# Two encoder layers on one core: attention scores laid in couples of neighbouring PSUM banks, with one maximum and one exponential over 1024 keys

## The chip, the cores and the metric

The kernel runs on one core of a Trainium2 chip. Five engines of that core work from queues of their own: TensorE (PE, with its weight loads shown as PEld) multiplies matrices and writes the results to PSUM; VectorE (DVE) and ScalarE (ACT) work by element and can read PSUM; GpSimd (POOL) works by element on SBUF alone; SyncE (SP) issues the DMAs. PSUM has eight banks here, and the kernel gives each a name and a task. The metric is the device time of one execution in microseconds, the median over several runs. The profile is one further execution, and its own time is its span, from the first instruction to the last.

## The reference

Two sequences, a prompt of 2048 tokens and a sample of 512, go through two layers with the same weights. Half of a layer's width is a pooling mixer, the other half differential attention with four heads of two softmax maps each. The change touches the attention:

```python
def block(qblk):
    s = jnp.einsum('bqhcd,bkhcd->bhcqk', qblk, k, preferred_element_type=jnp.float32) * scale
    p = jax.nn.softmax(s, axis=-1)
    a = p[:, :, 0] - lam * p[:, :, 1]
    return jnp.einsum('bhqk,bkhe->bqhe', a.astype(v.dtype), v)
```

So for each head, each query and each of the maps c = 0 and 1 there is a row of scores over all keys, its maximum, the exponentials, and their sum. The two maps are combined into one before they are multiplied with the values.

## The kernel before

**Stages of a layer.** First come the projections of most tokens (`project`, L238, matmuls at L277 and L249), then attention (`attention`, L393) with the remaining projections and the pooled half of the outputs as filling work, then the outputs (`phase3`, L736). Both layers run so. All engines except SP follow the order in which the program text issues their instructions; a wait inside a queue holds everything behind it.

**Banks.** `bank(tag)` (L71) hands out PSUM tiles in turn: four banks "sc", two "tr", one "ot", one "mm". "sc" serves the projections, the attention's scores and the output products. A bank is taken again when every reader of its last contents is done.

**An attention step** (the loop at L591 to L663) handles four jobs. A job is 128 queries against 512 keys of one map: two matmuls (`score`, L439 and L440) into a bank. A prompt row of 2048 keys is thus four jobs, one whole step; a sample row of 512 keys is one job, and a step has four of them (two query tiles with two maps). While a step writes its scores, the four banks of the step before are exponentiated:

```python
for j in range(4):
    if j < len(jobs): score(*jobs[j])
    if j < len(pend): expo(*pend[j])
    if j < len(jobs): peak(*jobs[j])
    if j == 0: early = turn()
late = turn()
```

`score(j)` of this step takes the bank that `expo(j)` of the step before reads, so PE waits at L439 until ACT is done with it. `peak` (L450) takes the maximum of a bank on DVE into a column of `mx`, and after the fourth L453 makes the negated maximum `nm` of the row, which each exponential (L466) needs as its bias. The exponential also sums its elements; an accumulator read behind it stores the sum in `zc`.

**What else a step does.** `turn` (L596) flips two key tiles of an earlier, combined block with four transposes into a "tr" bank (`flip`, L491); it is called after the first score and after the fourth. `flip_split` splits what was flipped into a high part on ACT (L109, `ath`) and a low part on DVE (L114, `atl`), which frees the bank. `values` (L508) multiplies them with the values into the bank "ot"; those flipped late in the step before come before the filling products, those flipped early after them. `fill` (L1024) issues six products of the filling work. A query block (256 queries of a head) takes four steps, or one for the sample. When its last product is done, `finish` copies the bank "ot" on ACT (L516, `oc`), ahead of the late split; DVE multiplies it with the gate (L519, `mt`); in the next step its square is split (L524, L525 on ACT, L526 on DVE, `shl`), and two matmuls with ones (L533) sum the squares at the end of that step. `combine` (L468) runs on POOL once both maps of a query tile are exponentiated: adds over `zc` (L475), the factor, then a multiplication (L481) and an addition (L482) for each 1024 keys. In the last head the prompt's blocks alternate with the sample's (`blocks`, L566).

Of the kernel before, what the change touches and what calls it, by code (L numbers as in the profile page):

```python
# [20 lines left out]
P = 128  # L21
# [9 lines left out]
TB = 512  # L31
# [24 lines left out]
def trunk_kernel(ctx: ExitStack, tc: tile.TileContext, a, outs):  # L56
# [12 lines left out]
    taken = dict.fromkeys(BANKS, 0)  # L69

    def bank(tag):  # L71
        """the banks of a tag in turn"""
        taken[tag] += 1
        return psum.tile([P, TB], F32, name=f"{tag}{taken[tag] % BANKS[tag]}")
# [31 lines left out]
    def split(hi, lo, src, hi_eng, lo_eng):  # L106
        """hi = src rounded to float32r, lo = src - hi (exact)."""
        if hi_eng is nc.scalar:
            nc.scalar.activation(hi, src, AF.Copy)  # L109
        elif hi_eng is nc.gpsimd:  # L110
            nc.gpsimd.tensor_scalar(hi, src, 1.0, 0.0, op0=ALU.mult, op1=ALU.add)
        else:
            nc.vector.tensor_copy(hi, src)
        lo_eng.tensor_tensor(lo, src, f32(hi), op=ALU.subtract)  # L114
# [32 lines left out]
    def norm_block(l, c, st, tb, ht, xp, hts, early, free=lambda: True, more=None, slow=0):  # L147
        """h of 512 tokens, transposed and split, and their rotary tables; yields between
        small steps"""
# [78 lines left out]
    def load_w(raw, p, hi_eng, lo_eng, later=None):  # L228
        """half the rows of the weights of 256 projection columns, split"""
# [8 lines left out]
    def project(st, tb, kind, pair, w, ht, p, tag, halfway):  # L238
        """a pair of projection chunks for a block of tokens; yields between small steps"""
# [44 lines left out]
    def evacuate(st, sl, kind, pair, sub, ps, cs, raws, p):  # L284
        """what follows on a projection chunk, a small step at a time"""
# [36 lines left out]
    def stream(l, jobs, nxt, hts, p, hook, later):  # L322
        """the projections of a layer: each job is a pair of chunks for some blocks; a
        block yields None between small steps and a chunk's tail; True ends a job"""
# [21 lines left out]
    def pool_block(c, st, tb, u_p, t_p, tag):  # L346
        """the pooled channels of 512 tokens; yields between small steps"""
# [45 lines left out]
    def attention(c, p, po, fill):  # L393
        """software-pipelined: a step fills four banks with scores while the four of the
        step before are exponentiated and finished blocks are multiplied with the values"""
# [38 lines left out]
        def score(s, ch):  # L434
            ps = bank("sc")
            q, m = s["b"]["q"], s["m"]
            ts = slice(s["qt"] * P, (s["qt"] + 1) * P)
            kk = s["b"]["ks"][m][ch // 2][:, ch % 2 * TB : (ch % 2 + 1) * TB]
            nc.tensor.matmul(ps, lhsT=q[:, m, 0, ts], rhs=kk, start=True, stop=False)  # L439
            nc.tensor.matmul(ps, lhsT=q[:, m, 1, ts], rhs=kk, start=False, stop=True)  # L440
            s["ps"].append(ps)

        def peak(s, ch):
            if s["nch"] == 1:
                s["nm"] = small.tile([P, 1], F32, name="nm")
                nc.vector.tensor_reduce(s["nm"], s["ps"][ch], axis=AX.X, op=ALU.max, negate=True)
                return
            if ch == 0:
                s["mx"] = small.tile([P, 4], F32, name="mx")
            nc.vector.reduce_max(s["mx"][:, ch : ch + 1], s["ps"][ch], axis=AX.X)  # L450
            if ch == s["nch"] - 1:
                s["nm"] = small.tile([P, 1], F32, name="nm")
                nc.vector.tensor_reduce(s["nm"], s["mx"][:, : s["nch"]], axis=AX.X, op=ALU.max, negate=True)  # L453

        def expo(s, ch):
            m = s["m"]
            if ch == 0 and m == 0:
                s["b"]["z"][s["qt"]] = small.tile([P, 2, 4], F32, name="zc", bufs=16)
            if s["nch"] == 1:
                if s["qt"] == 0:  # L460
                    s["b"][f"e{m}"] = p[f"e{m}"].tile([P, EH], F32, name=f"e{m}")
                s["e"].append(s["b"][f"e{m}"][:, s["qt"] * TB : (s["qt"] + 1) * TB])
            elif ch % 2 == 0:
                s["e"].append(p[f"e{m}"].tile([P, EH], F32, name=f"e{m}"))
            dst = s["e"][ch // 2][:, ch % 2 * TB : (ch % 2 + 1) * TB]
            nc.scalar.activation(dst, s["ps"][ch], AF.Exp, bias=s["nm"], accum_out=s["b"]["z"][s["qt"]][:, m, ch : ch + 1])  # L466

        def combine(b, qt):  # L468
            s0, s1 = b["sets"][2 * qt], b["sets"][2 * qt + 1]
            nch = s0["nch"]  # L470
            z, w = b["z"][qt], nch // 2
# [12 lines left out]
        def flip(b, unit):  # L484
            """two key tiles of a query block, keys onto the partitions"""
# [43 lines left out]
        def squares(b, sq, shl):  # L529
            """the sums of the squares, on all partitions"""  # L530
# [5 lines left out]
        def scales(b, sq, ps):  # L536
            """per query and head, the factor of its normalisation"""
# [28 lines left out]
        def blocks():  # L566
            """the last prompt head in turn with the sample's heads"""
# [23 lines left out]
        while True:  # L591
# [21 lines left out]
            for j in range(4):  # L613
                if j < len(jobs):
                    score(*jobs[j])
                if j < len(pend):
                    expo(*pend[j])
                if j < len(jobs):
                    peak(*jobs[j])
# [53 lines left out]
    def load_wout(l, p, wo, ks, raws, pools):  # L673
        """output weights, split"""
# [30 lines left out]
    def pooled_outputs(wo, p):  # L705
        """the pooled channels' share of the outputs, a token tile after the other"""
# [20 lines left out]
    def drop(q):  # L727
        """a step of the first of a queue of generators"""
# [3 lines left out]
    def each(q):  # L732
        """a step of all of them"""
        q[:] = [g for g in q if next(g, q) is not q]

    def phase3(l, wo, scaling, pairs, kept, es, nxt):  # L736
        """the outputs; what is left of them is returned for the next layer's begin"""
# [9 lines left out]
        def load(st, t):  # L747
            """what a token tile needs, and its scales on the diagonals of matrices"""
# [419 lines left out]
```

## Time and profile before

| | |
|---|---|
| median of three runs | 3195.07 us (3192.13 to 3199.23) |
| the profiled execution, its span | 3198.0 us |
| mean granted TensorE clock | 0.990 |
| first layer: projections, attention | to about 630 us, to about 1440 us |
| second layer: attention | about 2220 to 3025 us |

The page sums busy times over the whole span, so its shares mix stages with different limits. Of an engine's group of instructions it gives the sum, the mean of one, and the idle time in front of them with what ended it. The timeline gives start and length of single instructions, and in brackets the idle time of their engine before them. A matmul's length is modelled to the end of its way through the array, so neighbours overlap: the spacing of their starts is the time that one really takes of the engine.

### The profile page before, as it was taken

Reading aid. Unit: us, or ns where it says so; the run is one execution under the profiler, and the core shown is the slowest. Engines: PE = TensorE matmul, PEld = TensorE weight load, DVE = VectorE, ACT = ScalarE, POOL = GpSimd, SP = SyncE. Lnnn points to the kernel's source line nnn. Section 1 sums busy time; section 2 is a strip of 40 time slices with the busy share of each in tenths; the row PEclk is TensorE's granted clock in tenths of the full one; section 3 lists DMA queues with packets and bytes.
Section 4 is the critical chain, followed back from the end, with each engine's and each line's share of the span. In section 5 each row is a group of like instructions: output and inputs, shape, how many; then the busy total and the mean of one; then the engine's idle time right before and its main releaser. Section 6 shows DMA issues by size and latency. Waiting matters only on the chain. (4 is left out here: it accounts for less than half of the span.)

```text
span 3198.0 us, 48570 instructions
## 1 busy us (share of the span) xinstructions
PE 3088.4 (97%) x16936; PEld 2601.0 (81%) x16936; DVE 2174.8 (68%) x3289; ACT 1751.7 (55%) x3995; POOL 1856.8 (58%) x2058
## 2 busy tenths in 40 slices
PE   8999999999999999998899999999999999999998
PEld 6898888778887888887688888887788878888876
DVE  3354255588888887877834543555888988877767
ACT  3244233377777777773333442333777777777722
POOL 1000122288998888888820001222989888888888
PEclk9999999999999999999999999999999999999999
DMA  5354357643424334436754544577434243353367
GB/s 199 116 158 145 129 159 207 193 133 98 124 63 133 111 105 133 126 100 237 265 183 118 158 137 137 165 202 214 117 90 122 64 139 112 93 154 111 103 216 241
DMA packets 298902, 464.55 MB, mean 145 GB/s; under 512 B 26144, under 2 KB 180768, under 8 KB 298656
## 3 DMA queue, kind: packets, MB, share of 16 engines
q1 hardware_dynamic: 298656, 461.44, 48.2%
q8 instruction: 134, 2.20, 0.3%
q14 instruction: 112, 0.92, 0.1%
HBM read 293.57 MB, written 167.77 MB: 144 GB/s over the span
## 5 line engine op out<-in xcount | busy, mean ns | idle before, releaser
L450 DVE TENSOR_REDUCE mx<-sc 128x1 f32<-128x512 f32 x1024 | 650.4, 684 | 189.1 <-PE sc L440 187.1
L466 ACT ACTIVATE e<-sc,nm 128x512 f32<-128x512 f32 x1088 | 733.1, 694 | 44.0 <-DVE nm L453 40.0
L482 POOL TENSOR_TENSOR e<-e,e 128x1024 f32<-128x1024 f32 (+1 forms) x288 | 666.2, 2313 | 24.0
L277 PE MATMUL sc<-hth,wh 128*128 128x512 f32 x1408 | 556.0, 395 | 0.0
L277 PE MATMUL sc<-htl,wh 128*128 128x512 f32 x1408 | 554.6, 394 | 0.0
L277 PE MATMUL sc<-hth,wl 128*128 128x512 f32 x1408 | 552.8, 393 | 0.0
L109 ACT ACTIVATE ath<-tr 128x512 fp32r<-128x512 f32 x544 | 327.9, 605 | 236.8 <-PE ot L508 193.5
L439 PE MATMUL sc<-ks,q 128*128 128x512 f32 x1024 | 432.9, 423 | 10.4 <-DMA ks<-ks_p 5.3
L440 PE MATMUL sc<-ks,q 128*128 128x512 f32 x1024 | 406.5, 397 | 0.0
L114 DVE TENSOR_TENSOR atl<-tr,ath 128x512 fp32r<-128x512 f32 x544 | 363.6, 682 | 46.5 <-ACT ath L109 46.3
L508 PE MATMUL ot<-ath,v 128*128 128x256 f32 x2176 | 370.1, 292 | 1.9 <-ACT oc L516 1.9
L491 PE MATMUL tr<-ident,e 128*128 128x128 f32 x2176 | 328.3, 275 | 21.7 <-DVE atl L114 21.3
L491 PEld LDWEIGHTS tr<-ident,e 128*128 128x128 f32 x2176 | 268.5, 141 | 97.9 <-DVE atl L114 34.1
L167 POOL TENSOR_TENSOR rs<-ss,mhalf 128x1 f32<-128x1 f32 x40 | 27.0, 676 | 551.9 <-DVE ss L165 551.8
L481 POOL TENSOR_SCALAR e<-e,nco 128x1024 f32<-128x1024 f32 (+1 forms) x288 | 328.0, 1139 | 15.0
L508 PEld LDWEIGHTS ot<-ath,v 128*128 128x128 f32 x2176 | 312.6, 190 | 22.4 <-ACT oc L516 2.7
L277 PEld LDWEIGHTS sc<-hth,wl 128*128 128x128 f32 x1408 | 264.7, 188 | 59.1
L277 PEld LDWEIGHTS sc<-hth,wh 128*128 128x128 f32 x1408 | 264.8, 188 | 58.5 <-POOL wl L114 0.3
L277 PEld LDWEIGHTS sc<-htl,wh 128*128 128x128 f32 x1408 | 264.9, 188 | 57.6 <-DVE htl L114 0.4
L439 PEld LDWEIGHTS sc<-ks,q 128*128 128x128 f32 x1024 | 194.4, 190 | 64.6 <-ACT e L466 30.8
L114 DVE TENSOR_TENSOR wl<-wr,wh 128x1024 fp32r<-128x1024 f32 x94 | 120.8, 1287 | 182.2 <-ACT wh L109 182.1
L466 ACT ACTIVATION_READ_ACCUMULATOR e<-sc,nm 128x1 f32 x1088 | 231.1, 212 | 0.0
(149 smaller groups left out, 5987.6 us busy)
## 6 DMA issues: line engine op xcount, KB each, us to landing
wr<-in_w_in SPq DMA_DIRECT2D x128, 512.0 KB, 4.2
q<-qs_p SPq DMA_DIRECT2D x128, 256.0 KB, 4.2
ks_p<-hl SPq DMA_DIRECT2D x64, 256.0 KB, 3.5
vs_p<-hl SPq DMA_DIRECT2D x128, 128.0 KB, 2.7
qs_p<-hl SPq DMA_DIRECT2D x64, 256.0 KB, 3.5
mp_p<-hl SPq DMA_DIRECT2D x32, 512.0 KB, 3.8
ks<-ks_p SPq DMA_DIRECT2D x64, 256.0 KB, 5.4
v<-vs_p SPq DMA_DIRECT2D x32, 512.0 KB, 5.5
```

Source lines behind the costliest of these rows:

```text
L109: nc.scalar.activation(hi, src, AF.Copy)
L114: lo_eng.tensor_tensor(lo, src, f32(hi), op=ALU.subtract)
L167: nc.gpsimd.tensor_tensor(rs, ss, mhalf[:, :1], op=ALU.pow)
L277: nc.tensor.matmul(ps, lhsT=w[k // 4][m][:, k % 4, ns], rhs=h[:, k, :], start=k + i == 0, stop=k == KT - 1 and i == 2)
L439: nc.tensor.matmul(ps, lhsT=q[:, m, 0, ts], rhs=kk, start=True, stop=False)
L440: nc.tensor.matmul(ps, lhsT=q[:, m, 1, ts], rhs=kk, start=False, stop=True)
L450: nc.vector.reduce_max(s["mx"][:, ch : ch + 1], s["ps"][ch], axis=AX.X)
L466: nc.scalar.activation(dst, s["ps"][ch], AF.Exp, bias=s["nm"], accum_out=s["b"]["z"][s["qt"]][:, m, ch : ch + 1])
L481: nc.gpsimd.tensor_scalar(x1[:, :n], x1[:, :n], nco, 0.0, op0=ALU.mult, op1=ALU.add)
L482: nc.gpsimd.tensor_tensor(x0[:, :n], x0[:, :n], x1[:, :n], op=ALU.add)
L491: nc.tensor.transpose(ps[:, j, qt * P : (qt + 1) * P], e[kt // 8][:, kt % 8 * P : (kt % 8 + 1) * P], ident)
L508: nc.tensor.matmul(b["ot"][:, :QB], lhsT=b["vs"][v][kt // 8][:, kt % 8, :], rhs=at[:, j, :], start=unit + i == 0, stop=kt == nkt - 1 and i ...
```

## The change

The four "sc" banks become two tiles of two neighbouring banks, `sc0` and `sc1`. `bank("sc")` returns a half of such a couple; a new couple is taken at every second call, and is free only when all readers of both old halves are done. The projections and the output products use the halves as they used banks.

In a step the jobs are handled by twos. Two scores are written, then the couple of the step before is exponentiated, then the maximum of the new couple is taken. For the prompt, maximum and exponential each read 1024 keys of both banks in one instruction; `mx` and `zc` have two columns instead of four, and `combine` adds once instead of twice. For the sample one maximum instruction gives the two maxima of a couple, and the exponentials stay at 512 keys each. The early flip now comes after the second score. The rest of the diff takes comment strings out.

```diff
+    couples = []
     def bank(tag):
-        taken[tag] += 1
-        return psum.tile([P, TB], F32, name=f"{tag}{taken[tag] % BANKS[tag]}")
+        n, taken[tag] = taken[tag], taken[tag] + 1
+        if tag != "sc":
+            return psum.tile([P, TB], F32, name=f"{tag}{n % BANKS[tag]}")
+        if n % 2 == 0:
+            couples[:] = [psum.tile([P, 2, TB], F32, name=f"sc{n // 2 % 2}")]
+        return couples[0][:, n % 2]
...
+        def peak(jobs):
+            s, ch = jobs[0]
+            both = s["ps"][ch]
             if s["nch"] == 1:
+                nm = small.tile([P, 2], F32, name="nm")
+                nc.vector.tensor_reduce(nm, both, axis=AX.X, op=ALU.max, negate=True)
+                for i, (s, _) in enumerate(jobs):
+                    s["nm"] = nm[:, i : i + 1]
                 return
...
-            nc.vector.reduce_max(s["mx"][:, ch : ch + 1], s["ps"][ch], axis=AX.X)
-            if ch == s["nch"] - 1:
+            nc.vector.reduce_max(s["mx"][:, ch // 2 : ch // 2 + 1], both.rearrange("p i n -> p (i n)"), axis=AX.X)
+            if ch == s["nch"] - 2:
...
+        def expo(jobs):
+            for s, ch in jobs:
...
+                    nc.scalar.activation(s["e"][0], s["ps"][0][:, m], AF.Exp, bias=s["nm"], accum_out=z)
+                elif ch % 2 == 0:
+                    s["e"].append(p[f"e{m}"].tile([P, EH], F32, name=f"e{m}"))
+                    src = s["ps"][ch].rearrange("p i n -> p (i n)")
+                    nc.scalar.activation(s["e"][-1], src, AF.Exp, bias=s["nm"], accum_out=z)
...
-            z, w = b["z"][qt], nch // 2
+            z, w = b["z"][qt], nch // 4
...
-            for j in range(4):
-                if j < len(jobs):
-                    score(*jobs[j])
-                if j < len(pend):
-                    expo(*pend[j])
-                if j < len(jobs):
-                    peak(*jobs[j])
+            for j in (0, 2):
+                if jobs:
+                    score(jobs[j : j + 2])
+                if pend:
+                    expo(pend[j : j + 2])
+                if jobs:
+                    peak(jobs[j : j + 2])
                 if j == 0:
                     early = turn()
```

More of the change, by code (lines that the diff above doesn't have):

```diff
@@ L432, in load_q, with score @@
             return q
[L434 to L443, printed above, removed]
+        def score(jobs):
+            for s, ch in jobs:
+                ps = bank("sc")
+                q, m = s["b"]["q"], s["m"]
+                ts = slice(s["qt"] * P, (s["qt"] + 1) * P)
+                kk = s["b"]["ks"][m][ch // 2][:, ch % 2 * TB : (ch % 2 + 1) * TB]
+                nc.tensor.matmul(ps, lhsT=q[:, m, 0, ts], rhs=kk, start=True, stop=False)
+                nc.tensor.matmul(ps, lhsT=q[:, m, 1, ts], rhs=kk, start=False, stop=True)
+                s["ps"].append(couples[0])
@@ L444, in peak @@
+        def peak(jobs):
+            s, ch = jobs[0]
+            both = s["ps"][ch]
             if s["nch"] == 1:
-                s["nm"] = small.tile([P, 1], F32, name="nm")
-                nc.vector.tensor_reduce(s["nm"], s["ps"][ch], axis=AX.X, op=ALU.max, negate=True)
+                nm = small.tile([P, 2], F32, name="nm")
+                nc.vector.tensor_reduce(nm, both, axis=AX.X, op=ALU.max, negate=True)
+                for i, (s, _) in enumerate(jobs):
+                    s["nm"] = nm[:, i : i + 1]
@@ L447, in peak @@
                 return
             if ch == 0:
-                s["mx"] = small.tile([P, 4], F32, name="mx")
-            nc.vector.reduce_max(s["mx"][:, ch : ch + 1], s["ps"][ch], axis=AX.X)
-            if ch == s["nch"] - 1:
+                s["mx"] = small.tile([P, 2], F32, name="mx")
+            nc.vector.reduce_max(s["mx"][:, ch // 2 : ch // 2 + 1], both.rearrange("p i n -> p (i n)"), axis=AX.X)
+            if ch == s["nch"] - 2:
                 s["nm"] = small.tile([P, 1], F32, name="nm")
-                nc.vector.tensor_reduce(s["nm"], s["mx"][:, : s["nch"]], axis=AX.X, op=ALU.max, negate=True)
@@ L455, in expo @@
[L455 to L466, printed above, removed]
+                nc.vector.tensor_reduce(s["nm"], s["mx"], axis=AX.X, op=ALU.max, negate=True)
@@ new lines, in expo @@
+        def expo(jobs):
+            for s, ch in jobs:
+                m = s["m"]
+                if ch == 0 and m == 0:
+                    s["b"]["z"][s["qt"]] = small.tile([P, 2, 2], F32, name="zc", bufs=16)
+                z = s["b"]["z"][s["qt"]][:, m, ch // 2 : ch // 2 + 1]
+                if s["nch"] == 1:
+                    if s["qt"] == 0:
+                        s["b"][f"e{m}"] = p[f"e{m}"].tile([P, EH], F32, name=f"e{m}")
+                    s["e"].append(s["b"][f"e{m}"][:, s["qt"] * TB : (s["qt"] + 1) * TB])
+                    nc.scalar.activation(s["e"][0], s["ps"][0][:, m], AF.Exp, bias=s["nm"], accum_out=z)
[3 more added lines that the diff above has]
+                    nc.scalar.activation(s["e"][-1], src, AF.Exp, bias=s["nm"], accum_out=z)
```

## The prediction

> **What bounds the kernel now.** I read the page first: the span, the busy times, the groups of the two instructions that the change merges.
>
> ```profile
> span 3198.0 us, 48570 instructions
> PE 3088.4 (97%) x16936; PEld 2601.0 (81%) x16936; DVE 2174.8 (68%) x3289; ACT 1751.7 (55%) x3995; POOL 1856.8 (58%) x2058
> ...
> L450 DVE TENSOR_REDUCE mx<-sc 128x1 f32<-128x512 f32 x1024 | 650.4, 684 | 189.1 <-PE sc L440 187.1
> L466 ACT ACTIVATE e<-sc,nm 128x512 f32<-128x512 f32 x1088 | 733.1, 694 | 44.0 <-DVE nm L453 40.0
> ...
> L466 ACT ACTIVATION_READ_ACCUMULATOR e<-sc,nm 128x1 f32 x1088 | 231.1, 212 | 0.0
> ```
>
> TensorE is the bound by its busy share, and the merged instructions lie on VectorE and ScalarE. The next view, busy time by window over two neighbouring attention steps (from one first score load to the next), says what that means here.
>
> ```profile
> 1130.58:1136.13 5.55, 5.55 (x37) 4.84 (x36) 3.93 (x7) 3.85 (x11) 5.38 (x4) 1.00 0.00 0
> 1136.13:1141.67 5.54, 5.54 (x36) 4.83 (x35) 4.21 (x8) 4.53 (x12) 3.30 (x6) 1.00 0.14 50
> ```
>
> The columns are length, then busy PE, weight loads, DVE, ACT, POOL. PE is busy 5.55 of 5.55 us, DVE 3.93, ACT 3.85. Time saved on DVE or ACT is worth nothing in such a step. It counts only where PE waits, so I read the waits of its weight loads next (total us, times, longest).
>
> ```profile
> PEld tr L491 <- DVE atl L114: 34.1, 49, 3.5
> PEld sc L439 <- ACT e L466: 30.8, 78, 1.7
> ...
> PEld tr L533 <- DVE shl L526: 23.6, 34, 2.3
> ```
>
> These 88 us are the waits that the change can touch: 2.8% of the span. It can shorten them, or add to the second.
>
> **The change, part by part.** The prices of a doubled instruction come from the groups that differ in size only.
>
> ```profile
> L109 ACT ACTIVATE woh<-wor 128x512 fp32r<-128x512 f32 x16 | 10.2, 639 | 0.0
> L109 ACT ACTIVATE woh<-wor 128x1024 fp32r<-128x1024 f32 x8 | 8.5, 1068 | 0.0
> L453 DVE TENSOR_REDUCE nm<-mx 128x1 f32<-128x4 f32 x256 | 40.3, 158 | 8.8
> L543 DVE TENSOR_REDUCE v<-sq 128x2 f32<-128x256 f32 x80 | 33.6, 420 | 7.2
> ```
>
> ACT: 512 more elements cost 1068-639 = 0.43 us, so an exponential of 1024 takes about 0.694+0.43 = 1.12. DVE: (684-158)/508 = 1.04 ns an element, so a maximum of 1024 takes 0.684+0.53 = 1.21. Against two of 512 that saves 0.27 and 0.16, and 512 accumulator reads go. No row reads two banks at once. The bounds are therefore no second fixed cost at all (these prices) and nothing saved (1.39 and 1.37). I take the first, whose rows have the same sizes. The change removes no matmul and no DMA. POOL loses one 0.2 us add for each combine.
>
> Now the latency, in the quiet step.
>
> ```profile
> 1132.27 1.89 DVE L450 TENSOR_REDUCE mx<-sc 128x1 f32<-128x512 f32 x3 [0.21 <-PE sc L440]
> ...
> 1132.54 0.39 PE L439 MATMUL sc<-ks,q 128*128 128x512 f32 x1
> ...
> 1132.76 0.40 PE L440 MATMUL sc<-ks,q 128*128 128x512 f32 x1
> ...
> 1134.11 0.60 ACT L109 ACTIVATE ath<-tr 128x512 fp32r<-128x512 f32 x1 [1.70 <-PE ot L508]
> ...
> 1134.19 0.16 DVE L453 TENSOR_REDUCE nm<-mx 128x1 f32<-128x4 f32 x1
> ...
> 1134.60 0.68 ACT L466 ACTIVATE e<-sc,nm 128x512 f32<-128x512 f32 x1
> ...
> 1135.17 0.20 ACT L466 ACTIVATION_READ_ACCUMULATOR e<-sc,nm 128x1 f32 x1
> ...
> 1136.13 0.19 PEld L439 LDWEIGHTS sc<-ks,q 128*128 128x128 f32 x1
> ```
>
> The last score ends at 1133.16. Today the first bank is free when the accumulator read ends, 1135.37, and PE returns at 1136.13: 0.76 us of cover. Afterwards the second maximum starts at 1133.20 and ends at 1134.41, the combined one at about 1134.61, the exponential starts at 1134.65, its accumulator read (0.57+0.43 later) ends at 1135.85. Cover 0.2 to 0.3 us: **no loss, but little left**. Behind the waiting score load stand all of PE's later flips and products, so a wait beyond the cover is lost whole.
>
> In one step of each query block a finished output (L516) comes between, and there the cover is too small.
>
> ```profile
> L516 ACT ACTIVATE oc<-ot 128x256 f32<-128x256 f32 x80 | 30.8, 385 | 110.4 <-PE ot L508 110.4
> ```
> ```profile
> 1139.45 0.40 PE L508 MATMUL ot<-atl,v 128*128 128x256 f32 x2
> ...
> 1139.89 0.39 ACT L516 ACTIVATE oc<-ot 128x256 f32<-128x256 f32 x1 [1.01 <-PE ot L508]
> ...
> 1140.17 0.59 ACT L109 ACTIVATE ath<-tr 128x512 fp32r<-128x512 f32 x1
> ...
> 1140.65 0.69 ACT L466 ACTIVATE e<-sc,nm 128x512 f32<-128x512 f32 x1
> ...
> 1141.22 0.21 ACT L466 ACTIVATION_READ_ACCUMULATOR e<-sc,nm 128x1 f32 x1
> 1141.31 0.70 ACT L466 ACTIVATE e<-sc,nm 128x512 f32<-128x512 f32 x1
> ...
> 1141.67 0.19 PEld L439 LDWEIGHTS sc<-ks,q 128*128 128x128 f32 x1
> ```
>
> PE's product, the copy and the split hold the exponential to 1140.65 whatever the maxima do. Its read ends at 1141.43 now, 1141.86 after; PE asks at 1141.67, and a load follows a release by 0.05 us (1254.39 to 1254.44, below). So PE waits 0.24. Of the 64 prompt blocks the 48 of the first three heads have this step, two of them in a stretch without cover: 46 x 0.24 = **11 us lost** (0 to 23 between the bounds: a read that ends as early as today, and a doubled fixed cost, 0.24+0.26 each).
>
> In the last head the step before is the sample's. It keeps exponentials of 512, and a couple is free only after both.
>
> ```profile
> 1253.77 0.19 PEld L439 LDWEIGHTS sc<-ks,q 128*128 128x128 f32 x1 [0.37 <-ACT e L466]
> ...
> 1254.16 0.23 ACT L466 ACTIVATION_READ_ACCUMULATOR e<-sc,nm 128x1 f32 x1
> ...
> 1254.44 0.19 PEld L439 LDWEIGHTS sc<-ks,q 128*128 128x128 f32 x1 [0.37 <-ACT e L466]
> ```
>
> PE already follows the exponentials here; only the fourth score comes behind the fourth exponential. Afterwards the third does too: two matmuls at the 0.23 us spacing of 1132.54 and 1132.76, 0.46 us, in 14 such steps: **6 us lost**.
>
> Where PE has few filling products the loop through ACT and DVE sets the pace already.
>
> ```profile
> 653.38 0.19 PEld L439 LDWEIGHTS sc<-ks,q 128*128 128x128 f32 x1
> ...
> 657.82 0.19 PEld L439 LDWEIGHTS sc<-ks,q 128*128 128x128 f32 x1 [0.33 <-ACT e L466]
> ```
>
> 4.44 us a step. After: release to third score load 0.05, four matmuls 0.12+3x0.23+0.40, maximum 0.04+1.21, combined one 0.04+0.16, second exponential 0.04+(0.66+0.43) later (0.66 from 1140.65 to 1141.31, the spacing today), its read's end 1.20 after that: 5.0. About ten steps in both layers lie so, each at 0 to 0.6: **5 us lost**. Losses: 22.
>
> Gains. Flips wait for their bank (L491). The first flip moves behind the second score, 2 x 0.23 = 0.46 us later on PE, while the splits that free banks come 0.25 later in quiet steps.
>
> ```profile
> 1102.89 0.35 PEld L491 LDWEIGHTS tr<-ident,e 128*128 128x128 f32 x3 [0.18 <-DVE atl L114]
> ```
>
> Some 17 waits of this size vanish (3 us), and twelve of 0.8 to 3.5 lose 0.2 to 0.5 each: **7 us gained** of 34 (0 to 15). The second gain is at the squares.
>
> ```profile
> L475 POOL TENSOR_TENSOR zc<-zc 128x4 f32<-128x4 f32 x128 | 30.2, 236 | 58.5 <-ACT e L466 58.5
> ```
> ```profile
> 1099.55 2.41 POOL L482 TENSOR_TENSOR e<-e,e 128x1024 f32<-128x1024 f32 x1
> ...
> 1100.17 2.06 DVE L526 TENSOR_TENSOR shl<-sq,shl 128x256 fp32r<-128x256 f32 x1
> ...
> 1102.29 0.19 PEld L533 LDWEIGHTS tr<-shl,ones 128*128 128x128 f32 x1 [0.64 <-DVE shl L526]
> ```
>
> The DVE subtraction of 256 elements takes 2.06 us: it ends 0.27 after POOL's add that began before it. POOL's chain of adds starts at the latest accumulator read (L475 waits for it), in the quiet step at 1134.60+3x0.66+0.77 = 1137.35 now and at 1134.65+1.09+1.20 = 1136.94 after, 0.4 us earlier, and is one add shorter (0.24), 0.6 in all; this subtraction starts about 0.25 later in its step, and the step itself 0.24 later. Most of the collision is then over. Of the 23.6 us some 6 lie after the last scores; of the rest I take three quarters: **13 us gained** (0 to 17, or below: a new collision costs 0.64 a block).
>
> Elsewhere the couples cost nothing: a chunk of the projections waits for the evacuation of the chunk three back, not four, with two chunks of 24 matmuls x 0.23 = 11 us of cover, and L782's products have 12 x 0.23 x 2 = 5.5 us. Without that cover it would be one 0.6 us evacuation a time. At the start of a layer's attention the third score, not the fourth, waits for the last evacuation of the projections: 0.2 us, twice, which is in the rounding.
>
> Sum: 22 lost, 20 gained, **+2 us** on the span of 3198.0, which stands 2.9 above the median of the runs. On the median 3195.1: **3197**.
>
> **The rivals.** *Faster: the relief of the engines arrives in full.* All waits on DVE above, less 9 us after the last scores, are 49; if two thirds go and the losses are half of mine, 11-33 = -22: 3173; with all losses 3184. For it: 68% DVE, backlogged in the steps with long waits. Against it: quiet steps have no DVE wait at all. The Trainium skill ("Advanced Engine Details and Errata", The Read-Write Bubble) advises 512 or 1024 elements and one instruction over several banks; no wider read is in this trace yet.
>
> *Slower: coarser release, and the collision stays.* If the subtraction starts inside POOL's add after the change too, the 13 us don't come: 3197+13 = 3210; if every one of the 46 blocks collides at 0.64, +29 more. It decides as soon as the subtraction starts before POOL's add ends. For it: both starts move by amounts of the same size, and only the difference counts. The Trainium skill ("Perfetto Trace Analysis", Optimizing Scalar/DVE Operations) says that engines that are not full but cause bubbles elsewhere are helped by breaking instructions up; the 0.76 us of cover agree with it, as merging takes 0.5 of them.
>
> *It doesn't do what it says*: a read over two banks pays twice. Then the 11 become 23, and of the quiet steps the two in each of 46 blocks that have no squares behind them lose what their cover of 0.28 lacks against 0.27+0.16: 92 x 0.15 = 14. 3197+26 = 3223. Against it: the accumulator read and the fixed cost are seen once for each instruction here, and 256 to 512 elements already cost by the element on DVE.
>
> **How the numbers follow.** A measurement of this kernel tells 0.2%, 6.4 us, from no change. My forecast, losses and gains that cancel, 3197: 0.41. Coarse release 0.29 and double price 0.05: slower 0.34. Full relief: faster 0.25. Both signs together hold more than the forecast, whose own range is 3189 to 3201. The 80% range reaches from the rival with all losses and a little beyond, 3180, to between the slower ones, 3218.
>
> **What would show it.** Right: 512 exponentials of 128x1024 at about 1.12 us, maxima at 1.21; PE's waits for e at L439 up from 30.8 by some 20 us, in steps with an L516; L533's waits for shl well down; period of the quiet step still 5.55. Wrong: the quiet step grows (cover misjudged); exponentials of 1.39 us; shl waits that grow (the POOL phase); or PE busy falling with no named wait.

## The result, and the profile after

The changed kernel takes 3477.36 us (median of 4 runs, 3470.42 to 3483.95), the kernel before in the same comparison 3195.49 us (4 runs, 3192.13 to 3199.23). The ratio is 1.0883, 95% interval 1.087 to 1.0897: **slower by 8.8%**, far outside the predicted 3180 to 3218. Two of the runs below, the maximum alone and the exponential alone, each had one slow execution among four (11330.82 and 11864.49 us); their ratios leave it out.

The line numbers of the changed kernel are some lines further down. Those used here: the projections' matmuls are L282 (L277 before) and, for the values, L254; the copies that take a projection chunk out of its bank L294, L301, L307 (all `ra`) and L263; the outputs' matmuls L796 (L782) with their evacuation L799; scores L446 and L447, maximum L461, exponential L480 (L476 for the sample), flips L505, copy of a finished output L530, squares L547.

First the head of the page of the changed kernel, with the groups of the two merged instructions.

```profile
span 3468.6 us, 47211 instructions
PE 3159.9 (91%) x16936; PEld 2629.2 (76%) x16936; DVE 2121.9 (61%) x2745; ACT 1663.7 (48%) x2971; POOL 1793.2 (52%) x1930
...
L461 DVE TENSOR_REDUCE mx<-sc 128x1 f32<-128x1024 f32 x512 | 622.0, 1222 | 248.9 <-PE sc L447 219.8
L480 ACT ACTIVATE e<-sc,nm 128x1024 f32<-128x1024 f32 x512 | 566.6, 1114 | 47.4 <-DVE nm L464 45.3
```

The span grew by 270.6 us. (The medians are 281.9 apart: the profiled execution of the changed kernel lies 6.9 us under its median and the span of the kernel before 2.9 over its own, so differences of the two profiles come out some 11 us small.) The merged instructions cost what was expected of them (1.222 and 1.114 us), VectorE, ScalarE and GpSimd all have less to do than before, and TensorE has the same 16936 matmuls. But TensorE stands idle for 3468.6 - 3159.9 = 308.7 us instead of 109.6, and the time in which any of its matmuls runs is 71.5 us longer.

Where is that? Busy time by window, cut at the first and last score of each layer: the columns are the window, its length, then busy time (and instructions) of PE, weight loads, DVE, ACT, POOL, the granted clock, the DMA share and GB/s. The kernel before:

```profile
0.00:633.00 633.00, 617.38 (x3097) 519.20 (x3098) 298.25 (x395) 223.16 (x356) 96.46 (x116) 1.00 0.54 163
633.00:1435.00 802.00, 779.37 (x4708) 665.93 (x4707) 665.64 (x1118) 603.83 (x1548) 687.91 (x765) 0.99 0.40 113
1435.00:2223.00 788.00, 763.42 (x3764) 633.46 (x3763) 422.94 (x524) 272.39 (x451) 238.06 (x261) 0.99 0.58 179
2223.00:3022.00 799.00, 776.20 (x4707) 663.94 (x4706) 662.20 (x1118) 603.31 (x1547) 687.35 (x763) 0.99 0.40 114
3022.00:3198.00 176.00, 151.99 (x668) 118.45 (x666) 125.78 (x135) 49.03 (x96) 146.96 (x156) 0.95 0.67 217
```

The changed kernel:

```profile
0.00:740.00 740.00, 640.60 (x3097) 524.18 (x3098) 294.01 (x395) 224.36 (x356) 93.23 (x116) 0.97 0.46 140
740.00:1550.00 810.00, 781.99 (x4709) 669.32 (x4708) 645.58 (x848) 558.41 (x1036) 673.02 (x703) 1.00 0.40 112
1550.00:2475.00 925.00, 802.53 (x3765) 649.85 (x3764) 412.82 (x523) 273.75 (x450) 223.86 (x259) 0.96 0.50 153
2475.00:3284.00 809.00, 781.41 (x4706) 668.88 (x4706) 646.56 (x848) 558.58 (x1036) 672.61 (x703) 1.00 0.40 112
3284.00:3468.00 184.00, 153.34 (x664) 116.97 (x662) 122.92 (x133) 48.65 (x95) 130.49 (x153) 0.95 0.63 207
```

The windows hold the same matmuls, within a few. Attention (the second and fourth) grew by 8 and 10 us. The first projections grew by 107, the stretch from the first layer's outputs to the second layer's scores by 137, the last outputs by 8. So **some 250 of the 270 us lie where the change merges nothing**; what reached these stages is only the new shape of the tiles that `bank("sc")` hands out.

The waits of the weight loads in the changed kernel (total us, times, longest) name them.

```profile
PEld sc L282 <- ACT ra L307: 83.2, 32, 7.0
PEld sc L282 <- ACT ra L301: 81.9, 36, 8.6
PEld sc L796 <- DVE y L799: 58.4, 39, 4.7
PEld sc L446 <- ACT e L480: 38.9, 89, 2.9
PEld tr L505 <- DVE atl L119: 33.4, 42, 3.1
PEld sc L282 <- ACT ra L294: 26.1, 20, 4.2
PEld sc L254 <- ACT ra L263: 24.8, 16, 3.5
PEld sc L446 <- ACT e L476: 11.8, 24, 0.6
PEld tr L547 <- DVE shl L540: 9.2, 12, 1.7
```

Before the change no projection matmul into an `sc` bank waited for `ra` or for `y`. Now L282 waits 32 + 36 + 20 = 88 times, 191.2 us in all, L254 24.8 us and L796 58.4 us: 274 us, against 24.3 us of another wait (L782 for hl) that these hide now. That difference, 250 us, is about the loss outside attention.

The number 88 says more. L282 has 3 x 1408 = 4224 matmuls into `sc` banks; at 24 a chunk that is 176 chunks, or 88 couples: **one wait for each couple**. In order of issue, 36 of the waits stand at the first matmul of a couple's second half, 24 at its second and 28 at its third; none stands in a first half. L796's 39 waits are all at the first matmul of a second half, out of 40 couples of 12 matmuls a half. One of them in the timeline (start, length, engine, line; in brackets the idle time before, and what ended it):

```profile
253.15 0.39 PE L282 MATMUL sc<-hth,wh 128*128 128x512 f32 x1
...
253.61 0.39 PE L282 MATMUL sc<-hth,wl 128*128 128x512 f32 x1
253.74 0.69 DVE L319 TENSOR_TENSOR t<-t,t 128x512 f32<-128x512 f32 x1
254.47 0.63 ACT L114 ACTIVATE hl<-t 128x512 fp32r<-128x512 f32 x1 [2.14 <-DVE t L319]
255.00 0.58 ACT L307 ACTIVATE ra<-sc 128x512 f32<-128x512 f32 x1
...
255.63 0.19 PEld L282 LDWEIGHTS sc<-hth,wh 128*128 128x128 f32 x1 [2.06 <-ACT ra L307]
```

The first half of a couple is complete at 254.00. Its evacuation `ra` stands in ScalarE's queue behind a split that waits for VectorE, and ends at 255.58. The second half is another bank, which nobody reads; yet TensorE starts on it only at 255.63. The list of the built program shows the same without any time: a matmul in the middle of a second half waits for a semaphore of ScalarE, whose queue has the evacuation of the same tile (number 368) there; the count that it waits for is the one that this evacuation brings. The two matmuls before it are issued ahead of the evacuation and need not wait, which is why the wait stands at the first, second or third matmul of a half.

```
93 L282 MATMUL sc_368<-htl,wh 128x512
94 L282 MATMUL sc_368<-hth,wl 128x512 [waits Activation_49]
...
24 L294 ACTIVATE ra_422<-sc1_368 128x512 [waits DMAHW0_49,PE_49]
```

**Theory.** A couple is one tile, and the program's order between writers and readers is kept by the tile: writing one half waits for the read of the other half, though these are two banks. In the projections and outputs, where the halves are filled one after the other and each is read out alone, every second chunk waits for the evacuation of the chunk just finished. **Rival A**: it is the coarser release that I had named (a couple comes free only when both halves are read). **Rival B**: the merged attention disturbs what comes after.

### The profile page after: what moved, and what is told of

Its sections match the earlier page's. It is cut to its first block, busy times and chain, and to the rows that moved or that the text cites. A ratio compares the mean times of both kernels' runs of the same rounds, so it can differ in the third digit from the quotient of the medians.

```text
span 3468.6 us, 47211 instructions
## 1 busy us (share of the span) xinstructions
PE 3159.9 (91%) x16936; PEld 2629.2 (76%) x16936; DVE 2121.9 (61%) x2745; ACT 1663.7 (48%) x2971; POOL 1793.2 (52%) x1930
## 5 line engine op out<-in xcount | busy, mean ns | idle before, releaser
L461 DVE TENSOR_REDUCE mx<-sc 128x1 f32<-128x1024 f32 x512 | 622.0, 1222 | 248.9 <-PE sc L447 219.8
L282 PE MATMUL sc<-hth,wh 128*128 128x512 f32 x1408 | 569.8, 405 | 67.9 <-ACT ra L307 36.4
L282 PE MATMUL sc<-hth,wl 128*128 128x512 f32 x1408 | 566.9, 403 | 44.6 <-ACT ra L307 25.3
L282 PE MATMUL sc<-htl,wh 128*128 128x512 f32 x1408 | 567.8, 403 | 41.2 <-ACT ra L301 27.4
L480 ACT ACTIVATE e<-sc,nm 128x1024 f32<-128x1024 f32 x512 | 566.6, 1114 | 47.4 <-DVE nm L464 45.3
L446 PE MATMUL sc<-ks,q 128*128 128x512 f32 x1024 | 436.5, 426 | 25.4 <-ACT e L480 16.6
L447 PE MATMUL sc<-ks,q 128*128 128x512 f32 x1024 | 405.2, 396 | 0.0
L282 PEld LDWEIGHTS sc<-hth,wh 128*128 128x128 f32 x1408 | 271.5, 193 | 141.7 <-ACT ra L307 43.2
L282 PEld LDWEIGHTS sc<-hth,wl 128*128 128x128 f32 x1408 | 271.2, 193 | 116.3 <-ACT ra L307 28.7
L282 PEld LDWEIGHTS sc<-htl,wh 128*128 128x128 f32 x1408 | 271.3, 193 | 109.4 <-ACT ra L301 30.9
L505 PE MATMUL tr<-ident,e 128*128 128x128 f32 x2176 | 327.6, 275 | 20.0 <-DVE atl L119 19.5
L505 PEld LDWEIGHTS tr<-ident,e 128*128 128x128 f32 x2176 | 267.9, 141 | 98.3 <-DVE atl L119 33.4
L796 PE MATMUL sc<-woh,hl 128*128 128x512 f32 x640 | 214.1, 416 | 46.1 <-DVE y L799 41.1
L446 PEld LDWEIGHTS sc<-ks,q 128*128 128x128 f32 x1024 | 193.9, 189 | 76.9 <-ACT e L480 38.9
```

Source lines behind the costliest of these rows:

```text
L282: nc.tensor.matmul(ps, lhsT=w[k // 4][m][:, k % 4, ns], rhs=h[:, k, :], start=k + i == 0, stop=k == KT - 1 and i == 2)
L461: nc.vector.reduce_max(s["mx"][:, ch // 2 : ch // 2 + 1], both.rearrange("p i n -> p (i n)"), axis=AX.X)
L480: nc.scalar.activation(s["e"][-1], src, AF.Exp, bias=s["nm"], accum_out=z)
L505: nc.tensor.transpose(ps[:, j, qt * P : (qt + 1) * P], e[kt // 8][:, kt % 8 * P : (kt % 8 + 1) * P], ident)
L796: nc.tensor.matmul(ps, lhsT=lhsT, rhs=w[:, ns], start=i == 0, stop=i == len(todo) - 1)
```

## The experiments

**Where it sits: each part of the change alone.** The first run keeps couples in attention only. The score banks get a pool of their own, opened anew as single banks or as couples at the borders of attention.

```diff
+        if scores["kind"] == "single":
+            return scores["pool"].tile([P, TB], F32, name=f"sb{n % 4}")
         if n % 2 == 0:
-            couples[:] = [psum.tile([P, 2, TB], F32, name=f"sc{n // 2 % 2}")]
+            couples[:] = [scores["pool"].tile([P, 2, TB], F32, name=f"sc{n // 2 % 2}")]
...
+            lay("couple")
             scaling = attention(c, pa, po, fill)
+            lay("single")
```

> Couples in attention only; projections, poolings and outputs write single 512-wide banks again, as before the change. Theory (a couple is one tile, so matmuls into one half wait until the other half has been read out): the waits of L282 on ra (83.2 + 81.9 + 26.1 us after the change) and of L796 on y (58.4 us) go, the two projection stages fall back to some 634 and 613 us, and the time is about 3213 us (3195 + the 17.6 us that attention lost; 3205 to 3220). Rival A (the couples cost outside attention because a chunk must wait for an evacuation three back): the same time, so this run alone does not tell it from the theory. Rival B (the loss comes from attention or from memory laid out otherwise, and the projections only show it): over 3400 us.

Measured: 3223.29 us, ratio 1.0087 (1.0069 to 1.0105), 3 us above the expected range: attention costs more here than the 17.6 us of the one profile that the forecast went by. The opposite run is the kernel before with its old attention and single banks there, and couple tiles, never used as couples, everywhere else.

> The kernel before with its attention as it was (single banks, maxima and exponentials of 512 keys), but with couple tiles, unused as couples, for the projections, the poolings and the outputs. Theory (a write to one half waits for the read of the other half): 3195 + 107 + 118 + 20 + some 12 of the last outputs = about 3450 us (3430 to 3465), with the same waits of L282's twin on ra and of L796's twin on y in second halves. Rival (the loss needs the change in attention too, by the order of work it hands on): near 3195 us.

Measured: 3457.26 us, ratio 1.0813 (1.0798 to 1.0828). The two parts add up to within 7 us: 28 us from attention alone, 260 from the other stages alone, 282 from both. Rival B is out: the old attention with couples elsewhere shows the same waits to within a few per cent (its L293, L318, L312 and L798, L801 are the changed kernel's L282, L307, L301 and L796, L799).

```profile
PEld sc L293 <- ACT ra L318: 83.0, 32, 7.0
PEld sc L293 <- ACT ra L312: 82.3, 36, 9.0
PEld sc L798 <- DVE y L801: 58.1, 39, 4.7
```

**What it is: tile or release.** The next run keeps the couples in every stage. Outside attention only the order differs in which chunks take the four halves: the first halves of both couples, then the second halves.

```diff
+        if where["crossed"]:
+            if n % 4 < 2:
+                crossed[n % 2] = psum.tile([P, 2, TB], F32, name=f"sc{n % 2}")
+            return crossed[n % 2][:, n // 2 % 2]
         if n % 2 == 0:
```

> Couple tiles everywhere, but outside attention neighbouring chunks go crosswise: first halves of both couples, then second halves. Four banks, and a couple is still taken anew only when both of its halves are read. Theory (writes to one half wait for reads of the other): the chunk that follows an evacuation is in the other tile, so what waits is a chunk two later, a whole chunk (24 x 0.23 = 5.5 us) after the evacuation was queued: most of the 216 us of L282's waits go, 3213 to 3260 us. Rival A (coarse release of a couple): the release is coarser than in the changed kernel, the last half of a couple is read out just before it is needed, so the waits stay or grow: 3470 us or more, with the waits at a first half's first matmul.

Measured: 3228.43 us, ratio 1.0097 (1.008 to 1.0114). What is left of the waits of the projections for `ra` (here L286 and L258), from the crossed run:

```profile
PEld sc L286 <- ACT ra L311: 6.5, 4, 2.1
...
PEld sc L286 <- ACT ra L305: 4.6, 2, 2.4
PEld sc L258 <- ACT ra L267: 2.5, 2, 1.3
```

13.6 us instead of 216.0. The release of a couple is as coarse as ever, or coarser, so rival A predicted no less than 3470 and falls. With neighbouring chunks in different tiles the read of one chunk has the whole next chunk (5.5 us) to itself, and that is enough. At the outputs, where a chunk is only 12 products (2.8 us), it is not quite: L800, the outputs' matmuls of the crossed run, still waits 31.1 us, where the changed kernel has 58.4 for y and the kernel before 24.3 for hl; the view names no releaser for these loads, and for 17.5 us of the matmuls behind them it names y.

**Within attention: which half of the merge costs.** Two runs start from the single-outside run and take one merge back: the maximum alone over 1024 keys (exponentials of 512 each), and the exponential alone.

```diff
-                    src = s["ps"][ch].rearrange("p i n -> p (i n)")
-                    nc.scalar.activation(s["e"][-1], src, AF.Exp, bias=s["nm"], accum_out=z)
+                if s["nch"] > 1:
+                    z = s["b"]["z"][s["qt"]][:, m, ch : ch + 1]
+                    dst = s["e"][ch // 2][:, ch % 2 * TB : (ch % 2 + 1) * TB]
+                    nc.scalar.activation(dst, s["ps"][ch][:, ch % 2], AF.Exp, bias=s["nm"], accum_out=z)
```

> As the single-outside run, but in attention only the maximum runs over 1024 keys; the exponentials run over 512 each (four partial sums again). Theory: the 0.24 us of a step with a finished output come from the long exponential, behind which the copy of the output delays the next one, so they go (11 us), the exponentials of 0.69 us come twice 0.69 - 1.11 = 0.27 us per pair dearer on a ScalarE that is half idle, and the loss of the short-fill stretches is halved: 3195 to 3205 us. Rival: the maximum over 1024 alone sets the loss (the exponential must wait for a 1.22 us maximum instead of 0.68): as slow as with both, 3213 us.

```diff
-            nc.vector.reduce_max(s["mx"][:, ch // 2 : ch // 2 + 1], both.rearrange("p i n -> p (i n)"), axis=AX.X)
+            for i in range(2):
+                nc.vector.reduce_max(s["mx"][:, ch + i : ch + i + 1], both[:, i], axis=AX.X)
```

> As the single-outside run, but in attention only the exponential runs over 1024 keys; the maxima run over 512 each. Theory: the steps with a finished output keep their 0.24 us (11 us), the short-fill stretches get part of theirs back, as the last maximum starts after the last score's bank and takes 0.68 us: 3205 to 3213 us. Rival: the maximum is what costs, and this one is back at 3195 us.

Measured: 3257.53 us (1.019, 1.0173 to 1.0207) and 3233.11 us (1.0111, 1.0094 to 1.0128). Both miss: **neither is faster than both merges together** (3223.29), and the maximum alone is clearly slower. For that one, I had forgotten my own theory. As long as two banks are one tile, the first score of a couple waits for the second exponential, and two of 0.691 us end later than one of 1.115. The waits for e say so, and those of the squares for shl grow nearly as much; single-outside first, then maximum only:

```profile
PEld sc L457 <- ACT e L491: 40.0, 93, 2.9
PEld tr L558 <- DVE shl L551: 12.6, 14, 1.7
```
```profile
PEld sc L457 <- ACT e L493: 56.6, 99, 2.5
PEld tr L560 <- DVE shl L553: 26.1, 39, 2.4
```

So with couples in place merging the exponential pays (34 us, 3257.53 against 3223.29). Merging the maximum as well may pay a little (10 us, 3233.11 against 3223.29), but the intervals of these two runs overlap. Neither run says what single banks would do; that is the order-only run below.

**The 0.24 us of a step with a finished output.** Two ways to take the copy `oc` out of the way of the long exponential. First onto VectorE, in the single-outside run and, as a control, in the kernel before:

```diff
-            nc.scalar.activation(oc, ot[:, :QB], AF.Copy)
+            nc.vector.tensor_copy(oc, ot[:, :QB])
```

> As the single-outside run (3223 us), and the copy of a finished output out of its bank (the oc line) runs on VectorE, no longer on ScalarE between two long exponentials. Theory (the 0.24 us of 46 steps with a finished output and part of the 0.49 us of the 14 sample steps come from this copy delaying a long exponential): these steps go back to 5.55 us, 11 to 18 us less than the single-outside run, 3205 to 3212 us. Rival (the second exponential is late because its maximum ends late, whatever stands in ScalarE's queue): the steps keep 5.79 us, and the time stays at 3223 us.

> Control: the kernel before with the same copy on VectorE. Its exponentials of 0.69 us left room for the copy, so theory expects no change, 3190 to 3202 us. If the copy on ScalarE cost the kernel before something too, it would be under 3185 us.

Measured: 3240.9 us (1.0133, 1.0119 to 1.0147) and 3219.56 us (1.0069, 1.0055 to 1.0082). Both miss, and the control says why the pair can't decide: the move by itself costs the kernel before 23 us. In such a step of the run, from the timeline, the exponential is early, at 988.37 in a step that began at 984.30 (4.07 us in, where the single-outside run has 4.53), but the products of the next block wait until the copy, now behind the maxima and a split in VectorE's queue, has left their bank:

```profile
988.37 1.11 ACT L491 ACTIVATE e<-sc,nm 128x1024 f32<-128x1024 f32 x1
988.85 0.41 DVE L541 COPY oc<-ot 128x256 f32<-128x256 f32 x1
...
989.38 0.53 PEld L533 LDWEIGHTS ot<-ath,v 128*128 128x128 f32 x4 [0.39 <-issue]
```

A cleaner way leaves the copy on ScalarE and changes only its place: the split of the second flip, whose data are there earlier, goes ahead of it.

```diff
-            for g in finishing:
-                next(g)
             if late:
                 flip_split(late[2])
                 flipped.append(late)
             for g in finishing:
                 next(g)
+            for g in finishing:
+                next(g)
```

> As the single-outside run (3223 us), with one order changed: the split of the second flip of a step (ath on ScalarE, atl on VectorE) is issued ahead of the copy oc of a finished output, not behind it. In the single-outside run oc waits 1.49 us for its products in front of that ath and the exponential, which starts 4.53 us into such a step although its maximum is there at 4.02. Theory (ScalarE's queue makes the long exponential late in these steps, and its end releases the couple 0.24 us late): the exponential starts some 0.3 to 0.4 us earlier, these 46 steps go back to 5.55 to 5.6 us without burdening VectorE, and the time falls by 8 to 15 us, to 3208 to 3215 us. Rival (something else of these steps, such as the later maximum or the copy's place on whichever engine, costs the 0.24): 3220 us or more.

> Control: the kernel before with the same order of split and copy. Its first bank is free after 0.69 us of exponentials, 5.21 us into a step of 5.55, so theory expects no gain from an earlier exponential: 3190 to 3200 us.

Measured: 3207.33 us (1.0035, 1.0022 to 1.0049), 16 us less than the single-outside run and just past the expected range, and for the control 3197.1 us (1.0007, 0.9998 to 1.0016), the kernel before unchanged. The same step in the timelines, the single-outside run first (its step begins at 977.56):

```profile
981.33 0.39 ACT L541 ACTIVATE oc<-ot 128x256 f32<-128x256 f32 x1 [1.49 <-PE ot L533]
...
981.61 0.59 ACT L125 ACTIVATE ath<-tr 128x512 fp32r<-128x512 f32 x1
982.09 1.12 ACT L491 ACTIVATE e<-sc,nm 128x1024 f32<-128x1024 f32 x1
...
983.35 0.19 PEld L457 LDWEIGHTS sc<-ks,q 128*128 128x128 f32 x1 [0.15 <-ACT e L491]
```

With the split first (its step begins at 972.57):

```profile
976.10 0.60 ACT L125 ACTIVATE ath<-tr 128x512 fp32r<-128x512 f32 x1 [1.25 <-PE ot L533]
...
976.59 0.38 ACT L541 ACTIVATE oc<-ot 128x256 f32<-128x256 f32 x1
976.86 1.12 ACT L491 ACTIVATE e<-sc,nm 128x1024 f32<-128x1024 f32 x1
...
978.13 0.19 PEld L457 LDWEIGHTS sc<-ks,q 128*128 128x128 f32 x1
```

The exponential starts 4.29 us into the step instead of 4.53, and the next score load comes after 5.56 us, without a wait, instead of 5.79. The 0.24 us are ScalarE's order in front of a long exponential, as the prediction said.

In the sample's steps half of the loss stayed (5.80 us from score load to score load; 5.54 before, 6.03 after). One more run gives each of the sample's score sets a maximum of its own:

```diff
-                nm = small.tile([P, 2], F32, name="nm")
-                nc.vector.tensor_reduce(nm, both, axis=AX.X, op=ALU.max, negate=True)
                 for i, (s, _) in enumerate(jobs):
-                    s["nm"] = nm[:, i : i + 1]
+                    s["nm"] = small.tile([P, 1], F32, name=f"nm{i}")
+                    nc.vector.tensor_reduce(s["nm"], both[:, i], axis=AX.X, op=ALU.max, negate=True)
```

> The run with the split first (3207 us, 1024 keys an instruction), with the maxima of the sample's steps taken over 512 keys each, one per score set, so that its first exponential need not wait for both. Theory (in the sample's steps the 1.22 us maximum, after which 2 x 0.69 us of exponentials follow, is what is left of the loss: 14 steps of 5.80 for 5.54 us and 14 of 9.50 for 9.16): up to 0.3 us in each, 4 to 8 us, 3199 to 3204 us. Rival (the couple is released by its last exponential, which waits for the second maximum either way): 3206 us or more.

Measured: 3211.17 us, ratio 1.0053 (1.0033 to 1.0073): no gain. The steps keep 5.80 us, so the merged maximum does not set them. That fits the rival, release by the last exponential.

**Order without width.** The change also moved the first flip behind two scores. The kernel before, with single banks and 512 keys, and only that order:

```diff
-            for j in range(4):
-                if j < len(jobs):
-                    score(*jobs[j])
-                if j < len(pend):
-                    expo(*pend[j])
-                if j < len(jobs):
-                    peak(*jobs[j])
+            for j in (0, 2):
+                for job in jobs[j : j + 2]:
+                    score(*job)
+                for job in pend[j : j + 2]:
+                    expo(*job)
+                for job in jobs[j : j + 2]:
+                    peak(*job)
```

> The kernel before with single banks and instructions of 512 keys, and only the order of the change: two scores, two exponentials, two maxima, then the first flip. It tells the order from the width. Theory (the gains in attention, 11.5 to 5.9 us, 9.8 to 7.4 us and 7.7 to 5.6 us in the long steps, come from the flip behind two scores, the losses from the width): the long steps are short, the 0.24 us of the steps with a finished output stay away, 3165 to 3190 us. Rival (the gains come from less work on VectorE, 1222 for 2 x 684 ns): 3195 us or slower, because the second score must now wait for the second exponential.

> The order-only run (3189 us, 512 keys an instruction, single banks) with the split of the second flip ahead of the copy oc. With instructions of 512 keys neither kernel's steps with a finished output were late (5.55 us), and the control, the kernel before with this order, stayed where it was; so theory expects 3183 to 3192 us, no gain beyond the order-only run that could be told from none. Rival (the waits of the scores for e, 39.1 us there against 30.8 before, come from the copy ahead of the exponentials): under 3180 us.

Measured: 3189.15 us, ratio 0.9983 (0.9974 to 0.9992), and with the split first as well 3191.4 us, 0.9997 (0.9989 to 1.0006), no gain on top. The order-only run is the fastest kernel of the study, and the only one whose interval lies below the kernel before, by 0.17%; the other run with this order, which has the split first as well, doesn't repeat even that. Its waits show which gain belongs to which part.

```profile
PEld sc L439 <- ACT e L466: 39.1, 127, 1.4
PEld tr L491 <- DVE atl L114: 24.7, 31, 3.0
...
PEld tr L533 <- DVE shl L526: 23.6, 34, 2.3
```

The waits of the flips for `atl` fall from 34.1 to 24.7 us, so that gain is the order's. Those of the squares for `shl` stay at 23.6, the value of before; in the changed kernel they are 9.2, so that gain is the width's, and of the two widths the exponential's: 26.1 us with the maximum alone wide, 15.3 with the exponential alone. The DVE subtraction of the squares shows the same in its median length: 0.68 us before, 0.73 with the maximum alone wide, 0.42 with the exponential alone and with both. Of the long steps the order alone takes only a part, for instance 11.55 to 9.68 us where the changed kernel has 5.92.

All runs, in us:

| kernel | median | ratio to before (95%) |
|---|---|---|
| changed kernel | 3477.36 | 1.0883 (1.087 to 1.0897) |
| couples outside attention only | 3457.26 | 1.0813 (1.0798 to 1.0828) |
| couples in attention only | 3223.29 | 1.0087 (1.0069 to 1.0105) |
| couples everywhere, crossed | 3228.43 | 1.0097 (1.008 to 1.0114) |
| in attention only, maximum only | 3257.53 | 1.019 (1.0173 to 1.0207) |
| in attention only, exponential only | 3233.11 | 1.0111 (1.0094 to 1.0128) |
| in attention only, copy on VectorE | 3240.9 | 1.0133 (1.0119 to 1.0147) |
| before, copy on VectorE | 3219.56 | 1.0069 (1.0055 to 1.0082) |
| in attention only, split first | 3207.33 | 1.0035 (1.0022 to 1.0049) |
| the same, sample's maxima single | 3211.17 | 1.0053 (1.0033 to 1.0073) |
| before, split first | 3197.1 | 1.0007 (0.9998 to 1.0016) |
| before, order only | 3189.15 | 0.9983 (0.9974 to 0.9992) |
| before, order only, split first | 3191.4 | 0.9997 (0.9989 to 1.0006) |

## Why the prediction was wrong, point by point

**The step that failed** is the sentence "Elsewhere the couples cost nothing: a chunk of the projections waits for the evacuation of the chunk three back, not four, with two chunks of 24 matmuls x 0.23 = 11 us of cover". I asked when a couple comes free and never when its second half may be written. By the tile, the second half waits for the read of the first half, the chunk directly before: no cover at all. In its place the runs show 253 us (270.6 less attention's 17.6, from the first to the last score load of each layer): the couples outside attention alone bring 260 us, and taking them away there, or crossing them, leaves 28 or 33 us of the 282. The sentence's fallback was wrong in size too: "one 0.6 us evacuation a time". The 88 waits of L282 last 191.2 / 88 = 2.2 us in the mean and up to 8.6, since the evacuation also stands in ScalarE's queue, in the case shown behind a split that waits for VectorE. None of the rivals held this mechanism. The nearest, coarser release, looked at the reuse of a couple as well, and was priced in attention only.

**Right in mechanism and size.** The prices (1.114 for 1.12 us, 1.222 for 1.21). The quiet steps, 5.55 or 5.56 us after in 96 of the other 111 (the rest below). The steps with a finished output: 36 quiet steps of 5.55 grew by 0.24 us, as worked out, and the run with the split first took that away, in 34 of the 36, by the cause named. The sample's steps: 0.49 us where 0.46 was said, in 12 steps, but that size is partly luck: the split-first run shows that half of it was ScalarE's order and not the third score. The squares: `shl` waits from 23.6 to 9.2 us, 14 for the 13 forecast, and the subtraction in front of them shortened in its median from 0.68 to 0.42 us, as was said of a collision that is mostly over. The waits of the scores for e: 30.8 to 38.9 + 11.8 = 50.7 us, the 20 more that were named.

**Right in sign, wrong in size.** The stretches with few filling products: the 14 steps under 5.1 us lost 11.5 us, not 5 (the 4.44 us step became 5.22, not 5.0). The steps of 9.16 us between the sample's and the next scores grew by 0.25 each, 3.0 us, which I had not listed. The flips' 7 us did not come (34.1 to 33.4): the order alone gives them (24.7), but other steps grew by up to 2.2 us, so that the total stood still. What in the width took them back is open: with the maximum alone wide these waits are 27.2 us, with the exponential alone 30.0, with both 33.2. These three make 6.5 + 3.0 + 7 = 16.5 us, near the 15.6 by which attention came out above its forecast (+17.6 for +2). That agreement is loose, since the fifteen other steps that were quiet before grew by 14 us in sum and long ones shrank (11.55 to 5.92 us), neither of which the forecast had.

**The rivals of attention.** The full relief did not come. The double price of a two-bank read is out by 1.114 us. The remaining 0.35% of the split-first run against the kernel before was not divided further. The Trainium skill ("Perfetto Trace Analysis", Optimizing Scalar/DVE Operations) says that breaking up instructions of engines which are not full but hold others up may let the work be done sooner. With single banks no run tests it, as none has instructions of 1024 keys there, though the fastest runs are the ones with 512. With couples it did not hold for the exponential (3257.53 with it broken up, 3223.29 merged), and for the maximum the runs can't tell.

## What to carry to other kernels

When several banks are put into one tile so that one instruction may read them, look at every other user of that tile: here each write to one part then waited for reads of the other parts, and a ring of four banks became a ring of two. Give the wide tile only to the stage that reads it whole, or hand out its parts crosswise, so that neighbours in time lie in different tiles. And on an engine that is not the bound, a merge lengthens the last link before the next release; here its throughput gain was worth nothing in the steps that TensorE fills, and its place in the queue decided (0.24 us a step, won back by reordering two instructions).

## What the runs showed of the hardware that I had not expected

Of the 270.6 us, 71.5 are no idle time: the same 16936 matmuls keep TensorE busy longer. In the first window 3097 matmuls take 640.60 us at a granted clock of 0.97, against 617.38 at 1.00 before. The run with couples outside attention only has the lower clock there as well, the single-outside run has not:

```profile
0.00:740.00 740.00, 641.31 (x3081) 525.12 (x3082) 294.14 (x395) 223.50 (x355) 91.80 (x115) 0.97 0.46 139
```
```profile
0.00:632.00 632.00, 614.86 (x3100) 516.78 (x3100) 299.85 (x395) 223.92 (x358) 98.69 (x116) 1.00 0.54 164
```

So the lower clock comes and goes with the waits of the couples. The trace shows how: the granted clock is 1.00 or 0.50 and nothing between, and it is 0.50 in 28 stretches of 3.4 to 10.2 us (149.8 us in all; before, 13 with 64.8 us). Of these 28, 27 begin in a wait of TensorE of 1.4 us or more, or within 3.5 us of its end. And it is the long waits: 18 of the 23 over 2.5 us have such a stretch behind or in them, 5 of the 228 under 1.4 us (23 of 24 and 5 of 197 in the run with couples outside attention only). That the waits bring it fits the order in time, and taking the couples out there took it away. One such stretch, behind a wait of 3.84 us, with its window:

```profile
159.73 0.50 PE L282 MATMUL sc<-hth,wh 128*128 128x512 f32 x1 [3.84 <-ACT ra L307]
...
160.45 0.63 PE L282 MATMUL sc<-hth,wl 128*128 128x512 f32 x1
160.88 0.63 PE L282 MATMUL sc<-hth,wh 128*128 128x512 f32 x1
```
```profile
160.11:163.52 3.41, 3.41 (x10) 2.63 (x9) 0.41 (x1) 0.00 (x0) 0.00 (x0) 0.50 0.63 154
```

The matmuls there start 0.43 us apart instead of 0.23. By an estimate from the trace the clock makes 33 of the 71.5 us: TensorE is busy 117.4 us inside such stretches against 51.5 before, and half of the difference is lost. Another part is only in the count, since a matmul's record is 0.39 us long at a spacing of 0.23, and each of the 155 further breaks lays some 0.16 us of it bare, 25 us. The rest is open.

The Trainium skill ("Perfetto Trace Analysis", Matmul Optimizations) says that the matrix engine scales its power by utilization and that matmuls should run back to back; these clocks agree. The same page (Optimizing Tensor Performance, Matmuls) asks that independent groups of matmuls rotate through different banks, so that reading one out overlaps the next. Here they did rotate, and still waited 274 us: a bank of its own was not enough, it had to be a tile of its own.
